# A LoRA kernel that streams its input through SBUF: loads and stores regrouped into six parts of 2, 6, 8, 16, 16 and 16 tiles

## The chip, the core and the metric

The kernel runs on one core of one Trainium2 chip. The metric is device time in microseconds (us) of one execution; a lower one is better. The kernel before took 125.18 us, the median of 3 runs (125.13 to 125.36).

## The reference: what is computed

```python
def setup_inputs():
    batch, seq, d_model, r = 16, 512, 768, 16
    ...
        "x": np.random.randn(batch, seq, d_model).astype(np.float32),
        "A": np.random.randn(d_model, r).astype(np.float32) * 0.1,
        "B": np.random.randn(r, d_model).astype(np.float32) * 0.1,
        "scale": 0.5,
...
    lora = np.matmul(np.matmul(x, A), B)
    return (x + scale * lora).astype(np.float32)
```

The input x has 8192 rows of 768 float32 numbers, which is 25.17 MB, and the output has as many. Every byte of x is read once and every byte of the output is written once; A and B have 48 KB each.

## The kernel before, in words

**Tiles, parts and chunks.** The 8192 rows are 64 tiles of 128 rows. The whole of x stays in one SBUF tensor `xs` of 128 partitions by 64 tiles by 768 numbers. The result is added into `xs` in place, and the stores take it from there. `LOADS` (line 13) groups the tiles into eight loads of 2, 2, 4, 8, 8, 8, 16 and 16 tiles. `rows` (line 69) lays a group of n tiles out so that each partition holds n rows which follow each other in DRAM: a load of 16 tiles is 128 runs of 48 KB, one to a partition. `STORES` (line 14) has ten stores of 2, 2, 4, 8, 8, 8, 8, 8, 8 and 8 tiles in the order of the tiles. Each of the last four is half of a 16-tile group, so it is 128 runs of 24 KB that lie 48 KB apart in DRAM.

**The queue.** All loads and stores are issued by SyncE (SP) into one hardware queue, which is served in order by 16 DMA engines. SP issues loads 0 and 1, then waits until a patch of SBUF is cleared (`zeroed`), issues the loads of A and B, then loads 2 to 6. The last load waits for `prep` (line 116), since A and B are staged in its space (line 64). Then SP goes through the stores: each waits until VectorE has counted `added` up (line 122), so that its tiles are summed.

**The work of a chunk.** Computing goes in 16 chunks of 4 tiles.
- `narrowed` (line 85) casts a third of the chunk (256 of the 768 columns) from float32 to float16 into `xh`; VectorE does thirds 0 and 1, ScalarE third 2. It waits for the landing of each load that holds a tile of the chunk, the first time that its engine needs that load.
- `turned` (line 181): TensorE transposes `xh` into PSUM by matmuls with the identity, six times for a chunk.
- ScalarE copies each transposed piece out of PSUM into `xt` (line 136).
- `projected` (line 192): TensorE multiplies by A, and ScalarE scales the result into `yt` (line 140).
- `expanded` (line 200): TensorE multiplies `yt` by B, for one tile, into one of two PSUM buffers.
- `summed` (line 145): VectorE adds that to the tile in `xs`; after the last tile of each store it drains and counts `added`.

**Order on each engine.** It is written out by hand. TensorE's first chunk waits for `prep` between its first three transposes and its first projection (line 227); then a loop runs over the chunks, each with the expansion of the chunk before it between its own steps. VectorE first casts two thirds of chunk 0, then transposes A and makes the float16 copies of A and B, which end with `prep` (line 165); in each later round it casts thirds 0 and 1 of the next chunk and sums the four tiles of the chunk before. ScalarE casts third 2 of the next chunk after the six copies of this one. POOL waits at the end until all stores have landed (line 129).

Of the kernel before, what the change touches and what calls it, by code (L numbers as in the profile page):

```python
# [9 lines left out]
MM_DT = mybir.dt.float16  # L10


LOADS = [2, 2, 4, 8, 8, 8, 16, 16]
STORES = [2, 2, 4, 8, 8, 8, 8, 8, 8, 8]

CHUNK = 4

# [2 lines left out]
def kernel(  # L20
# [8 lines left out]
    nc = tc.nc  # L29
    fp32 = mybir.dt.float32  # L30
    add = mybir.AluOpType.add
    P = 128

    x2 = x.flatten_outer_dims()
    out2 = out.flatten_outer_dims()
    T, D = x2.shape
    R = A.shape[1]
    NT = T // P
# [3 lines left out]
    NX = 3  # L42
    W = 2 * P
    NB = D // 32
    assert D % W == 0 and sum(LOADS) == NT == sum(STORES)
    n_splits = [(n0, min(512, D - n0)) for n0 in range(0, D, 512)]
    sc = float(scale)

    sb = ctx.enter_context(tc.tile_pool(name="sb", bufs=1))
    ps = ctx.enter_context(tc.tile_pool(name="ps", bufs=1, space=bass.MemoryType.PSUM))  # L50

    xs = sb.tile([P, NT, D], fp32, name="xs")
    ident = sb.tile([P, P], MM_DT, name="ident")
    a_mm = sb.tile([P, ND, R], MM_DT, name="a_mm")
    b_mm = sb.tile([R, D], MM_DT, name="b_mm")
    xh = [sb.tile([P, CHUNK, W], MM_DT, name=f"xh{u}") for u in range(NU)]
    xt = [sb.tile([P, CHUNK * P], MM_DT, name=f"xt{j}") for j in range(ND)]
    yt = sb.tile([R, CHUNK * P], MM_DT, name="yt")
    xt_ps = [ps.tile([P, CHUNK * P], fp32, name=f"xt_ps{b}") for b in range(NX)]
    yt_ps = ps.tile([R, CHUNK * P], fp32, name="yt_ps")  # L60
# [2 lines left out]

    room = NT - LOADS[-1]
    a_rows = xs[0:32, room, 0 : 32 * R].rearrange("b (a r) -> b a r", r=R)
    a_t = xs[0:32, room + 1, 0 : 32 * R].rearrange("a (r b) -> a r b", r=R)
    b_f32 = xs[0:R, room + 2, :]

    def rows(t2, t0, n):
        return t2[ds(t0 * P, n * P), :].rearrange("(p s) d -> p s d", s=n)  # L70

    with tc.tile_critical():  # L72
        names = "zeroed ident a b a_t prep fed0 fed1 fed2 turned got proj y lora freed added".split()
        S = {k: nc.alloc_semaphore(name=f"s_{k}") for k in names}
        landed = [nc.alloc_semaphore(name=f"s_load{i}") for i in range(len(LOADS))]
        stored = nc.alloc_semaphore(name="s_stored")
        part_of = [i for i, n in enumerate(LOADS) for _ in range(n)]

        def load(i):
            t0, n = sum(LOADS[:i]), LOADS[i]  # L80
            nc.sync.dma_start(out=xs[:, t0 : t0 + n, :], in_=rows(x2, t0, n)).then_inc(landed[i], 16)
# [3 lines left out]
        def narrowed(engine, c, u):  # L85
            for i in sorted({part_of[c * CHUNK + s] for s in range(CHUNK)}):
                if (engine.engine, i) not in known:
                    known.add((engine.engine, i))
                    engine.wait_ge(landed[i], 16)
            src = xs[:, ds(c * CHUNK, CHUNK), ds(u * W, W)]  # L90
            if engine is nc.scalar:
                i = engine.copy(out=xh[u], in_=src)  # L92
            else:
                i = engine.tensor_copy(out=xh[u], in_=src)  # L94
            i.then_inc(S[f"fed{u}"], 1)
# [6 lines left out]
            out=ident, in_=ident, compare_op=mybir.AluOpType.not_equal, fill=1.0,  # L102
# [8 lines left out]
            out=a_rows[0:NB, :, :], in_=A.rearrange("(b a) r -> b a r", a=32)  # L111
        ).then_inc(S["a"], 16)
        nc.sync.dma_start(out=b_f32, in_=B).then_inc(S["b"], 16)
        for i in range(2, len(LOADS) - 1):
            load(i)
        nc.sync.wait_ge(S["prep"], 1)
        load(len(LOADS) - 1)
        done = 0
        for k, n in enumerate(STORES):
            i = part_of[done]  # L120
            t0, w = sum(LOADS[:i]), LOADS[i]
            nc.sync.wait_ge(S["added"], k + 1)
            piece = slice(done - t0, done - t0 + n)
            nc.sync.dma_start(
                out=rows(out2, t0, w)[:, piece, :], in_=xs[:, done : done + n, :]
            ).then_inc(stored, 16)
            done += n

        nc.gpsimd.wait_ge(stored, 16 * len(STORES))


        narrowed(nc.scalar, 0, 2)
        for c in range(NC):
            for j in range(ND):
# [2 lines left out]
            if c + 1 < NC:  # L137
# [3 lines left out]
                out=yt, in_=yt_ps, func=mybir.ActivationFunctionType.Copy, scale=sc  # L141
# [8 lines left out]
            if k + 1 in ends:  # L150
                nc.vector.drain().then_inc(S["added"], 1)  # L151

        ends = {sum(STORES[: i + 1]) for i in range(len(STORES))}
        nc.vector.sem_inc(S["freed"], 2)
        narrowed(nc.vector, 0, 0)
        narrowed(nc.vector, 0, 1)
# [110 lines left out]
```

## Time and profile before

| what | value |
|---|---|
| median of 3 runs | 125.18 us |
| the profiled execution: its own time | 125.31 us |
| its span in the trace | 123.5 us |
| VectorE busy / TensorE matmul busy / ScalarE busy | 80.2 / 84.3 / 76.2 us |
| DMA packets, bytes, mean rate | 2662, 50.45 MB, 408 GB/s |
| first load issued / first store issued | 0.94 us / 21.39 us |
| last store issued / landed | 101.2 us / 122.5 us |

The profile shows one execution, with times from the start of its span. A DMA instruction on SP is short, since it only issues; the transfer is seen in the DMA rows and in the time from issue to landing. The DMA share of a stretch is the time that the packets starting in it took, as a share of the 16 engines. A packet here is one run of one partition, so a packet of 48 KB that starts near the end of a stretch counts wholly in that stretch, and single stretches of a microsecond swing around their mean. In a list of waits, "A <- B" says that A waited for B.

### The profile page before, as it was taken

Reading aid. Unit: us, or ns where it says so; the run is one execution under the profiler, and the core shown is the slowest. Engines: PE = TensorE matmul, PEld = TensorE weight load, DVE = VectorE, ACT = ScalarE, POOL = GpSimd, SP = SyncE. Lnnn points to the kernel's source line nnn. Section 1 sums busy time; section 2 is a strip of 40 time slices with the busy share of each in tenths; the row PEclk is TensorE's granted clock in tenths of the full one; section 3 lists DMA queues with packets and bytes.
Section 4 is the critical chain, followed back from the end, with each engine's and each line's share of the span. In section 5 each row is a group of like instructions: output and inputs, shape, how many; then the busy total and the mean of one; then the engine's idle time right before and its main releaser. Section 6 shows DMA issues by size and latency. Waiting matters only on the chain. (4 is left out here: it accounts for less than half of the span.)

```text
span 123.5 us, 1804 instructions
## 1 busy us (share of the span) xinstructions
PE 84.3 (68%) x608; PEld 39.7 (32%) x608; DVE 80.2 (65%) x102; ACT 76.2 (62%) x129; POOL 1.1 (1%) x7
## 2 busy tenths in 40 slices
PE   0024986999999999999999999999999420000000
PEld 0022342444445444454444544445444100000000
DVE  0049208888999999999899999999977770000000
ACT  0047598469889898898988989889896100000000
POOL 3000000000000000000000000000000000000000
PEclk9999999589999999999999999999999975555555
DMA  3999999999999699899889999999999999999990
GB/s 86 414 396 426 477 398 454 422 406 469 414 509 477 302 496 493 382 401 477 288 366 448 434 477 398 446 438 398 477 398 446 438 398 485 390 454 438 390 414 16
DMA packets 2662, 50.45 MB, mean 408 GB/s; under 512 B 316, under 2 KB 316, under 8 KB 868
## 3 DMA queue, kind: packets, MB, share of 16 engines
q1 hardware_dynamic: 2660, 50.43, 96.4%
q14 instruction: 2, 0.02, 0.0%
HBM read 25.26 MB, written 25.17 MB: 408 GB/s over the span
## 5 line engine op out<-in xcount | busy, mean ns | idle before, releaser
L147 DVE TENSOR_TENSOR xs<-xs,lo_ps 128x768 f32<-128x768 f32 x64 | 58.1, 950 | 5.5 <-PE lo_ps L205 4.8
L136 ACT CAST xt<-xt_ps 128x512 f16<-128x512 f32 x96 | 52.4, 577 | 10.1 <-PE xt_ps L186 8.4
L186 PE MATMUL xt_ps<-ident,xh 128*128 128x128 f16 x384 | 34.4, 229 | 8.6 <-PEq L179 8.6
L194 PE MATMUL yt_ps<-xt,a_mm 128*16 128x512 f16 x96 | 32.9, 396 | 1.8 <-PEq L179 1.6
L94 DVE CAST xh<-xs 128x1024 f16<-128x1024 f32 x32 | 22.0, 689 | 15.3 <-DMA xs<-in_x_dram 13.1
L186 PEld LDWEIGHTS xt_ps<-ident,xh 128*128 128x128 f16 x384 | 23.0, 102 | 26.9 <-issue 26.9
L205 PE MATMUL lo_ps<-b_mm,yt 16*128 16x512 f16 (+1 forms) x128 | 26.6, 324 | 5.4 <-PEq L179 3.5
L92 ACT CAST xh<-xs 128x1024 f16<-128x1024 f32 x16 | 16.8, 1048 | 0.0
L205 PEld LDWEIGHTS lo_ps<-b_mm,yt 16*128 16x128 f16 x128 | 9.6, 92 | 15.2 <-issue 9.5
L194 PEld LDWEIGHTS yt_ps<-xt,a_mm 128*16 128x16 f16 x96 | 7.1, 87 | 17.8 <-issue 13.0
L140 ACT ACTIVATE yt<-yt_ps 16x512 f16<-16x512 f32 x16 | 9.4, 587 | 2.6 <-PE yt_ps L194 2.6
L92 ACT ACT_TABLE_LOAD x1 | 1.3, 1283 | 7.8 <-DMA xs<-in_x_dram 7.8
L159 DVE STREAM_TRANSPOSE xs<-xs 32x512 f32<-32x512 f32 x1 | 1.0, 1037 | 0.0
L163 DVE CAST a_mm<-xs 32x96 f16<-32x96 f32 x4 | 0.9, 231 | 0.1
L165 DVE CAST b_mm<-xs 16x768 f16<-16x768 f32 x1 | 0.5, 548 | 0.0
L98 POOL MEMSET xs<- 32x512 f32 x1 | 0.5, 514 | 0.5 <-SPq L72 0.5
L101 POOL TENSOR_SCALAR_AFFINE_SELECT ident<-ident 128x128 f16<-128x128 f16 x1 | 0.3, 292 | 0.2 <-POOL ident L99 0.2
L99 POOL MEMSET ident<- 128x128 f16 x1 | 0.2, 194 | 0.0
L248 POOL MEMSET const-bfloat16-1.0<- 128x1 bf16 x1 | 0.1, 101 | 0.0
L248 POOL MEMSET const-uint8-127<- 128x1 uint8 x1 | 0.1, 101 | 0.0
L248 POOL MEMSET const-float32-0.0<- 128x1 f32 x1 | 0.1, 98 | 0.2 <-issue 0.2
L248 POOL MEMSET const-float32-1.0<- 128x1 f32 x1 | 0.1, 98 | 0.0
## 6 DMA issues: line engine op xcount, KB each, us to landing
out_dram<-xs SPq DMA_DIRECT2D x7, 3072.0 KB, 29.4
xs<-in_x_dram SPq DMA_DIRECT2D x2, 6144.0 KB, 48.0
xs<-in_x_dram SPq DMA_DIRECT2D x3, 3072.0 KB, 22.3
xs<-in_x_dram SPq DMA_DIRECT2D x2, 768.0 KB, 5.3
xs<-in_x_dram SPq DMA_DIRECT2D x1, 1536.0 KB, 8.8
out_dram<-xs SPq DMA_DIRECT2D x2, 768.0 KB, 44.2
out_dram<-xs SPq DMA_DIRECT2D x1, 1536.0 KB, 41.5
xs<-in_A_dram SPq DMA_DIRECT2D x1, 48.0 KB
```

Of the source, the lines that this page charges most:

```text
L92: i = engine.copy(out=xh[u], in_=src)
L94: i = engine.tensor_copy(out=xh[u], in_=src)
L98: nc.gpsimd.memset(a_rows, 0.0).then_inc(S["zeroed"], 1)
L136: nc.scalar.copy(out=xt[j], in_=xt_ps[j % NX]).then_inc(S["got"], 1)
L140: nc.scalar.activation(out=yt, in_=yt_ps, func=mybir.ActivationFunctionType.Copy, scale=sc).then_inc(S["y"], 1)
L147: nc.vector.tensor_tensor(out=xs[:, k, :], in0=xs[:, k, :], in1=lo_ps[k % 2], op=add).then_inc(S["freed"], 1)
L159: nc.vector.transpose(out=a_t, in_=a_rows.rearrange("b a r -> b r a")).then_inc(S["a_t"], 1)
L163: nc.vector.tensor_copy(out=a_mm[ds(32 * k, 32), :, :], in_=a_tv[:, k, :, :])
L165: nc.vector.tensor_copy(out=b_mm, in_=b_f32).then_inc(S["prep"], 1)
L186: i = nc.tensor.matmul(xt_ps[j % NX][:, ds(s * P, P)], xh[u][:, s, ds(h * P, P)], ident, start=True, stop=True,)
L194: i = nc.tensor.matmul(yt_ps, a_mm[:, j, :], xt[j], start=(j == 0), stop=(j == ND - 1))
L205: i = nc.tensor.matmul(lo_ps[s % 2][:, ds(n0, w)], yt[:, ds(s * P, P)], b_mm[:, ds(n0, w)], start=True, stop=True,)
```

## The change

- The tiles are grouped into six parts of 2, 6, 8, 16, 16 and 16 tiles. In each part a partition holds as many rows as the part has tiles, all next to each other in DRAM.
- There are seven loads: 2, 6, 8, 8, 8, 16 and 16 tiles. Part 3 (tiles 16 to 31) is loaded as two halves of 8 tiles, each 128 runs of 24 KB that lie 48 KB apart. The first chunk's four tiles come with loads 0 and 1 as before, and load 1 now has 6 tiles in place of 2. A and B are still issued after load 1, and the last load still waits for `prep`.
- There are six stores, each of a whole part, in the order 3, 0, 1, 2, 4, 5. The first (tiles 16 to 31) waits until four parts are summed, tiles 0 to 31; the stores of parts 0, 1 and 2 follow it without a wait; parts 4 and 5 wait for their own sums.
- VectorE drains and counts `added` six times in place of ten.
- ScalarE gets a first instruction: when the identity is made, it copies one column of it to a small tile that nothing reads.

```diff
-LOADS = [2, 2, 4, 8, 8, 8, 16, 16]
-STORES = [2, 2, 4, 8, 8, 8, 8, 8, 8, 8]
+PARTS = [2, 6, 8, 16, 16, 16]
+LOADS = [2, 6, 8, 8, 8, 16, 16]
+STORES = [3, 0, 1, 2, 4, 5]
...
+    first = sb.tile([P, 1], MM_DT, name="first")
...
+    starts = [sum(PARTS[:i]) for i in range(len(PARTS))]
+
     def rows(t2, t0, n):
-        return t2[ds(t0 * P, n * P), :].rearrange("(p s) d -> p s d", s=n)
+        i = max(i for i in range(len(PARTS)) if starts[i] <= t0)
+        part = t2[ds(starts[i] * P, PARTS[i] * P), :].rearrange("(p s) d -> p s d", s=PARTS[i])
+        return part[:, ds(t0 - starts[i], n), :]
...
-        done = 0
-        for k, n in enumerate(STORES):
-            i = part_of[done]
-            t0, w = sum(LOADS[:i]), LOADS[i]
-            nc.sync.wait_ge(S["added"], k + 1)
-            piece = slice(done - t0, done - t0 + n)
+        summed_parts = 0
+        for i in STORES:
+            t0, n = starts[i], PARTS[i]
+            if i + 1 > summed_parts:
+                summed_parts = i + 1
+                nc.sync.wait_ge(S["added"], summed_parts)
             nc.sync.dma_start(
-                out=rows(out2, t0, w)[:, piece, :], in_=xs[:, done : done + n, :]
+                out=rows(out2, t0, n), in_=xs[:, t0 : t0 + n, :]
             ).then_inc(stored, 16)
-            done += n
-
         nc.gpsimd.wait_ge(stored, 16 * len(STORES))
 
 
+        nc.scalar.wait_ge(S["ident"], 1)
+        nc.scalar.copy(out=first, in_=ident[:, 0:1])
         narrowed(nc.scalar, 0, 2)
...
-        ends = {sum(STORES[: i + 1]) for i in range(len(STORES))}
+        ends = {sum(PARTS[: i + 1]) for i in range(len(PARTS))}
```

More of the change, by code (lines that the diff above doesn't have):

```diff
@@ L44 @@
     NB = D // 32
-    assert D % W == 0 and sum(LOADS) == NT == sum(STORES)
+    assert D % W == 0 and sum(LOADS) == NT == sum(PARTS) and sorted(STORES) == list(range(len(PARTS)))
     n_splits = [(n0, min(512, D - n0)) for n0 in range(0, D, 512)]
```

## The prediction

> **What bounds the kernel now.** I read the page's DMA rows first, then the SP queue's instructions, then the time from issue to landing.
>
> ```profile
> DMA  3999999999999699899889999999999999999990
> q1 hardware_dynamic: 2660, 50.43, 96.4%
> ```
>
> The 16 DMA engines are busy from end to end: 96.4% of 123.5 us is 119.1 us. The digit 6 is no hole: the trace's packet records, laid end to end into 16 chains (the next packet starts within some 10 ns of the last one's end), have no gap over 30 ns between 2.0 and 120 us. The queue is served in order, so the chains are loads until about 62 us and stores after that. The issues show how far SP is ahead:
>
> ```profile
> 21.39 80.11 SPq L124 DMA_DIRECT2D out_dram<-xs  x10
> ...
> 60.96 0.33 SPq L124 DMA_DIRECT2D out_dram<-xs  x1
> ...
> 101.18 0.33 SPq L124 DMA_DIRECT2D out_dram<-xs  x1
> ```
>
> The first store is issued at 21.39 us and lands 44.5 us later, at 65.9, since all loads are ahead of it. The sixth (tiles 24 to 31) is issued at 60.96, the last at 101.18; that one lands 21.3 us later, at 122.5, and the span ends 1.04 us after it. So computing is 21 us ahead at the end, and what counts is the number of bytes, the rate, and whether an engine ever finds its queue empty. The last question is where this change acts.
>
> **When the sixteen engines leave the loads.** By the chains, twelve end their last load packet at 61.7 to 62.3 us, two at 62.7, one at 63.0, and the last at 63.86. From there to the last store packet takes 58.27 us on an ordinary chain (62.173 to 120.434). Two chains end late, at 122.03 and 122.12. One is that which left the loads at 63.86. The other left them early, at 61.9 or before, but is slow while storing: its 24 KB packets take 945 to 1001 ns against 912, until 95.5 us, when computing is nearly over. Its stores take about 60.14 us (61.893 to 122.030).
>
> **The start of the work.** Moved loads act here.
>
> ```profile
> 7.75 1.28 ACT L92 ACT_TABLE_LOAD   x1 [7.75 <-DMA xs<-in_x_dram]
> 7.78 1.29 DVE L94 CAST xh<-xs 128x1024 f16<-128x1024 f32 x2 [7.78 <-DMA xs<-in_x_dram]
> ...
> 11.04 0.55 DVE L165 CAST b_mm<-xs 16x768 f16<-16x768 f32 x1
> ...
> 11.69 0.59 PE L194 MATMUL yt_ps<-xt,a_mm 128*16 128x512 f16 x1 [1.63 <-PEq L179]
> ...
> 18.90 0.69 DVE L94 CAST xh<-xs 128x1024 f16<-128x1024 f32 x1 [5.35 <-DMA xs<-in_x_dram]
> ```
>
> Chunk 0 starts at 7.78, when tiles 2 and 3 have landed. VectorE's casts and its work on A and B end with `prep` at 11.59 (3.81 us later), and TensorE's first projection starts at 11.69. Later VectorE is idle for 5.35 us, until tiles 8 to 15 land: that is the only slack in front. From then on computing runs at a fixed pace: the stores of 8 tiles are issued at 40.36, 50.66 and 60.96, 10.30 apart, or 5.15 us for a chunk, with ScalarE, TensorE and VectorE each over 90% busy in 20 to 60 us. A delay that is left at 20 us is still there at 60.
>
> **The change, part by part.**
>
> *Fewer, longer packets.* An ordinary chain's stores of 2, 4 and 8 tiles follow each other at 1.86, 3.65 and 7.27 us by their landings; a 16-tile load took 14.53. Twice the size costs twice the time but for 0.02 to 0.08 us a transfer. Stores before: 2 x 1.86 + 3.65 + 7 x 7.27 = 58.26; after: 1.86 + 5.46 (3.65 and 7.27 halved in between) + 7.27 + 3 x 14.53 = 58.18. Loads save 0.05 in the same way. Gain: 0.1 to 0.15 us, on the path. Whole runs in DRAM bring nothing more: 24 KB runs 48 KB apart (stores 7 to 10) land 7.27 apart, just as contiguous ones do (stores 4 to 6).
>
> *Load 1 of 6 tiles.* The four-tile load of before lands 8.8 us after its issue at 2.73, at 11.5; by then tiles 0 to 7 and A and B have passed. The 6-tile load ends with the same bytes less the 0.1 MB of A and B (0.23 us at 420 GB/s): 11.25. Chunk 0 starts 3.5 us later, `prep` comes at 15.1, the first projection at 15.2, chunk 1's transposes at 19.5 (16.02 before). Cover: VectorE now comes to tiles 8 to 15 at about 20.1, when they have lain there since 18.8, so 1.2 us of the 3.5 is left at that point. Chunk 1 then runs without that stall, in some 5.6 us against 7.2, and chunk 2 in 5.15 against 5.93 (the granted clock fell to 0.5 from 21.97 to 25.38 there), so chunk 3 starts at about 30.3 instead of 29.14. **Delay: 1.2 us**; from below 0.8 (a landing at 10.9), from above 2.5, since the warm-up is not certain: matmuls of 512 columns took 0.60 us up to 15.1 and 0.38 after, that is 3.4 us after 11.69. If the same step comes a whole stretch of 3.4 us later, rounds of 1.07 us stand for rounds of 0.64, 0.4 us for each us, 1.4 in all. I take 1.2, the value that repeats the row.
>
> *ScalarE's early copy.* It moves the table load of 1.28 us from 7.75 to about 2. Before, its copies ended at 11.55 beside `prep` at 11.59; after, projections wait for `prep` at 15.1 anyway, and the copies end about 14.2. Worth 0; without that cover, 1.28.
>
> *Four drains less.* 0.87 us is the longest (the last, which ends the chain of waits); in mid-work VectorE isn't the one that others wait for. Taken at 0, with 0 to 0.2 in favour.
>
> *The first store.* Four stores that stood in the queue from 21 to 51 us, and a fifth and a sixth, become one that SP holds until tile 31 is summed: 60.96 + 1.2 = 62.15 us. It is the longest wait, and behind it on SP stand three stores that need nothing. From issue to the first packet on an empty queue took 1.02 us at the start (0.94 to 1.96), so packets flow at **63.2 us**. Bounds: 0 if the queue were never empty, 1.3 with the fill seen at the start, where first packets took 0.4 to 0.9 us for 0.23. Most engines have had nothing to do since about 61.9: 1.3 us lost on each. The engine that left the loads at 63.86 loses nothing, and its last packet (2.78 us against 1.82, as stores of others ran beside it) should be shorter.
>
> On issuing early, the Trainium skill speaks against this change: "DMA: Bandwidth & Descriptors", Rules for kernel authors, would have a DMA issued early so that its fixed cost overlaps. Its figure of about 2.0 us of fixed cost is for the other descriptor path; with that for my 1.02 the sum would be an estimated 1 us later. The same section would join small transfers into large ones; here ten stores land back to back, so no fixed cost shows that joining could save.
>
> *The end.* Parts 0 to 2 follow at once. Part 4 is summed at 81.5 + 1.2, when the queue has work until 63.2 + 14.5 + 14.6 = 92.3; part 5 at 102.4, plus 1.0, with work until 106.8. Cover: 3.4 us; no second hole. Should the delay reach 4.6, it opens.
>
> **The sum.** The slow storing chain: 63.2 + 60.14 - 0.08 = 123.2 for its last packet, landing 0.42 later as before (122.03 to 122.45), span end 1.04 after that: 124.7. The profiled execution's own time stands 1.77 over its span (125.31 to 123.54): 126.4. It was 0.13 over the median: **126.3 us**, 0.9% slower.
>
> **Rivals.**
>
> 1. *The gap is taken from engines that had time to spare (faster).* The chain that left the loads at 63.86 set the end too, and for it the store was never late. If the slow storing chain is slow only in the profiled execution (its excess ends with computing, and the page can't tell the cause), all engines begin at 63.2 and end 58.2 later, at 121.4; landing 0.4 and 1.04 more: 122.85, which gives 124.5; with 0.1 to 0.2 for filling, **124.6 us**. For: by the chains, eleven engines are done by 120.6 us and have some 1.5 us to spare at the end. Against: equal profiled and unprofiled times, which fit the slow chain being always there too. It decides for faster as long as the first packet flows before about 63.8.
> 2. *It comes out even.* As rival 1, but the delay is 1.7 to 2.2 us from a late warm-up: the gap eats the spare 0.6 us. **125.2 us.**
> 3. *Clock lost in front as well.* Slow chain as in the forecast and a delay of 2.5: 126.3 + 1.3 = **127.6 us**; without the slow chain, 125.9.
> 4. *The regrouping does nothing*, because a lead of loads or compute I overlook keeps the queue full: 125.18 - 0.15 = **125.0 us**. Against: 60.96 against 61.9 leaves SP 0.9 us, less than the 1.02 from issue to packet even with no delay.
>
> **Chances and range.** Forecast and rival 3 (both slower): 0.42 and 0.16. Rival 1: 0.26. Rivals 2 and 4: 0.11 and 0.05. About 0.2%, 0.25 us, is what a measurement of this kernel can tell from no change. Rival 4 and half of the edges of rival 2 fall inside that: faster 0.28, same 0.14, slower 0.58. The range goes from rival 1's 124.6 less 0.1 to 127.4, which leaves out the worst of rival 3. The forecast's own range is 125.7 to 127.0.
>
> **What would show it.** Right: SP's first store at 62 to 63 us; the DMA rows with a hole there, of about 1 us on most engines; chunk 0's casts at 11.3; no wait of VectorE for tiles 8 to 15; the last store landing about 60.5 us after the first packet. Wrong: chains that end together at 121.4, with no slow one (rival 1); a first store before 61 (rival 4); a granted clock of 0.5 or 0.60 us matmuls beyond 19 us (rivals 2 and 3); a second hole at 104 to 107.

## The result, and the profile after

The changed kernel took 126.24 us, the median of 7 runs (126.09 to 126.84), against 125.29 us for the kernel before (7 runs, 125.11 to 125.83). The ratio is 1.0081, with a 95% interval of 1.0063 to 1.0099: slower by 0.8%. The profiled execution had a span of 125.1 us and took 126.84 us, 0.6 us above the median, which the reading has to allow for. The ratio of each experiment below is to executions of the kernel before taken beside it; a few executions (3 of 12 in one run) fell into a slower state at a lower granted clock, and the medians below count them while the ratios leave them out.

The page's DMA rows and the SP queue's instructions after the change:

```profile
DMA  3999999999999979989595995999899699959960
...
q1 hardware_dynamic: 1940, 50.43, 94.8%
```
```profile
62.70 40.75 SPq L131 DMA_DIRECT2D out_dram<-xs  x6
...
103.11 0.33 SPq L131 DMA_DIRECT2D out_dram<-xs  x1
```

1940 packets in place of 2660 moved the same 50.43 MB, and the engines' time is the same: 94.8% of 125.06 is 118.6 us, 96.4% of 123.54 was 119.1. What grew is the time beside it, from 4.4 to 6.5 us. The first store is now issued at 62.70 us. The digits 5 and 6 late in the row don't show where it went, since a 48 KB packet is counted where it starts. Single microseconds around the hole do (the last two columns are the engines' share and GB/s); first the changed kernel, then the two middle ones in the kernel before:

```profile
60.00:61.00 1.00, 1.00 (x9) 0.45 (x8) 0.74 (x2) 0.94 (x3) 0.00 (x0) 1.00 0.68 295
61.00:62.00 1.00, 1.00 (x9) 0.43 (x9) 1.00 (x2) 1.00 (x2) 0.00 (x0) 1.00 0.01 0
62.00:63.00 1.00, 0.86 (x13) 0.59 (x11) 0.86 (x2) 1.00 (x3) 0.00 (x0) 1.00 0.00 0
63.00:64.00 1.00, 1.00 (x9) 0.44 (x7) 1.00 (x2) 0.87 (x2) 0.00 (x0) 1.00 1.87 786
```
```profile
61.00:62.00 1.00, 0.99 (x5) 0.37 (x5) 0.98 (x2) 1.00 (x3) 0.00 (x0) 1.00 0.29 98
62.00:63.00 1.00, 1.00 (x10) 0.54 (x9) 1.00 (x2) 0.64 (x2) 0.00 (x0) 1.00 0.77 320
```

After the change no data packet starts from 61 to 63, then 16 of 48 KB at once; before, packets start in both microseconds. By the packet chains fourteen engines leave the loads at 61.3 to 62.1, the others at 62.3 and 62.8, and all begin to store at 63.54 to 63.69, 0.85 us or more after the issue: each was idle for 0.9 to 2.2 us. The list of waits puts it on VectorE's sums (lines 151 and 158 are the drain after them); the kernel before first:

```profile
SPq L124 <- DVEq L151: 86.0, 10, 10.0
```
```profile
SPq L131 <- DVEq L158: 84.0, 3, 47.0
```

There are three waits where there were ten, and one of 47.0 us. Their total, 86.0 before and 84.0 now, says nothing: SP waits all the time in both kernels, and only in one are the DMA engines out of work meanwhile.

The front, from the timeline, answers to the lines shown of before:

```profile
0.90 1.28 ACT L138 ACT_TABLE_LOAD   x1 [0.90 <-SPq L79]
...
11.54 1.29 DVE L101 CAST xh<-xs 128x1024 f16<-128x1024 f32 x2 [11.54 <-DMA xs<-in_x_dram]
...
15.44 0.58 PE L201 MATMUL yt_ps<-xt,a_mm 128*16 128x512 f16 x1 [1.62 <-PEq L186]
...
20.01 1.46 PE L193 MATMUL xt_ps<-ident,xh 128*128 128x128 f16 x12
...
21.08 0.69 DVE L101 CAST xh<-xs 128x1024 f16<-128x1024 f32 x1 [3.79 <-PE xt_ps L193]
...
30.88 0.84 PE L193 MATMUL xt_ps<-ident,xh 128*128 128x128 f16 x12
```

Chunk 0 starts at 11.54 in place of 7.78 and the first projection at 15.44 in place of 11.69. VectorE's idle time before the casts of chunk 2 (line 101) is now 3.79 us and ends with TensorE, no longer with the DMA. The twelve transposes at 20.01 took 1.46 us, those at 30.88 took 0.84: the TensorE clock came up at 21.76, later than in the trace of before (15.1). Chunk 3 starts 1.74 us later than before (30.88 to 29.14), and 62.70 is 1.74 later than 60.96: what is lost at 30 us arrives unchanged at the first store.

The last line is in the tail, the same view:

```profile
120.00:121.00 1.00, 0.00 (x0) 0.00 (x0) 0.00 (x0) 0.00 (x0) 0.00 (x0) 0.50 1.71 737
121.00:122.00 1.00, 0.00 (x0) 0.00 (x0) 0.00 (x0) 0.00 (x0) 0.00 (x0) 0.50 0.11 49
```

49 GB/s in a microsecond is one packet of 48 KB. Fifteen engines start their last packet from 120 to 121 (737 is 15 x 49.15), one starts its own after 121. It is the slowly storing chain: fifteen land by 122.49, the last at 124.02.

### The profile page after: what moved, and what is told of

The parts are those of the page before. It is cut to its first block, busy times and chain, and to the rows that moved or that the text cites. A ratio compares the mean times of both kernels' runs of the same rounds, so it can differ in the third digit from the quotient of the medians.

```text
span 125.1 us, 1795 instructions
## 1 busy us (share of the span) xinstructions
PE 84.3 (67%) x608; PEld 39.7 (32%) x608; DVE 80.3 (64%) x102; ACT 76.5 (61%) x130; POOL 1.2 (1%) x7
## 3 DMA queue, kind: packets, MB, share of 16 engines
q1 hardware_dynamic: 1940, 50.43, 94.8%
```

## The experiments

Theory: the loss is the hole between loads and stores, made by two things together: computing starts 3.6 to 3.8 us later, and the first store waits for tile 31. Rivals: the regrouping (whole 16-tile parts, the six-tile load) costs by itself; holding stores back costs by itself; engines have time to spare, so the hole is mostly free. Each edit is to the changed kernel unless said otherwise.

**Natural order.** The stores no longer wait for tile 31.

```diff
-STORES = [3, 0, 1, 2, 4, 5]
+STORES = [0, 1, 2, 3, 4, 5]
```

> The changed kernel with its six stores in the order of the tiles (0, 1, 2, 3, 4, 5), so that the first is issued at about 24 us and stands in the queue behind the loads. Theory (what costs is the hole between loads and stores): no hole, and the time is that of the kernel before less 0.1 us of packets: 125.0 to 125.3 us, although computing still starts 3.5 us later. Rival (whole 16-tile parts, or the six-tile load, cost by themselves): 126.2 us, as with the change.

Measured: 125.19 us, ratio to before 0.9989 (0.9975 to 1.0002). The SP queue's instructions:

```profile
23.26 79.47 SPq L131 DMA_DIRECT2D out_dram<-xs  x6
```

Computing starts as late as in the change (chunk 0's casts at 11.35) and it costs nothing, since the first store is in the queue at 23.26. Whole parts, the six-tile load and the late start by themselves cost nothing that shows; the first rival falls.

**The kernel before, with its stores held.** An edit to the kernel before:

```diff
-            nc.sync.wait_ge(S["added"], k + 1)
+            nc.sync.wait_ge(S["added"], max(k + 1, 6))
```

> The kernel before with one edit: its stores wait until 32 tiles are summed, and the first six are then issued together, at about 61 us. Theory: packets flow at 61.9 us, when most engines have just left the loads, so the hole is at most 0.2 us on the chain that stores slowly: 125.2 to 125.5 us. Rival (holding the stores back costs by itself, whenever it ends): 126.2 us or more.

Measured: 125.19 us, ratio 0.9986 (0.9972 to 1.0001). The SP queue's instructions:

```profile
59.65 40.55 SPq L124 DMA_DIRECT2D out_dram<-xs  x10
```

The first store was issued at 59.65 us, before any engine had left the loads, so no hole came. Holding the stores back costs nothing that shows as long as it ends in time; the second rival falls.

**The front of before, stores still held.**

```diff
-PARTS = [2, 6, 8, 16, 16, 16]
-LOADS = [2, 6, 8, 8, 8, 16, 16]
-STORES = [3, 0, 1, 2, 4, 5]
+PARTS = [2, 2, 4, 8, 16, 16, 16]
+LOADS = [2, 2, 4, 8, 8, 8, 16, 16]
+STORES = [4, 0, 1, 2, 3, 5, 6]
```

> The changed kernel with the first eight tiles as parts of 2, 2 and 4 again, and seven stores of whole parts, still with tiles 16 to 31 first. Theory: computing starts at 7.8 us again, the first store is issued at 61 us instead of over 62, and 1 us comes back: 125.1 to 125.5 us. Rival (the order of the stores, or whole 16-tile parts, cost): 126.2 us.

Measured: 124.96 us, ratio 0.998 (0.9955 to 1.0006); first store at 59.66. As the theory has it.

**Only the load of part 1 undone.** Parts and stores stay; part 1 is loaded in pieces of 2 and 4 tiles.

```diff
-LOADS = [2, 6, 8, 8, 8, 16, 16]
+LOADS = [2, 2, 4, 8, 8, 8, 16, 16]
```

> The changed kernel with parts and stores as they are, but part 1 loaded in two pieces of 2 and 4 tiles, so that chunk 0 can start at 7.8 us again. Theory (the front's delay, handed on to the held first store, is the whole loss): 124.8 to 125.2 us, with the first store issued at 59.7 to 61 us. Rival (something else of the change costs, which the front of before in the run with seven stores had hidden): 125.6 us or more.

Measured: 125.05 us, ratio 0.9977 (0.9964 to 0.999), so 0.2% faster than before and, by the two ratios, 1.0% faster than the change: the whole loss is gone. The SP queue's instructions, and the same single microseconds:

```profile
59.89 1.78 SPq L131 DMA_DIRECT2D out_dram<-xs  x3
```
```profile
61.00:62.00 1.00, 1.00 (x11) 0.56 (x10) 1.00 (x2) 0.64 (x2) 0.00 (x0) 1.00 1.27 541
62.00:63.00 1.00, 1.00 (x9) 0.53 (x9) 0.98 (x2) 0.89 (x3) 0.00 (x0) 1.00 0.57 246
```

Packets start in both stretches in which the changed kernel had none. The first store comes 2.81 us earlier than in the change, and the profiled time falls by 1.79 (126.84 to 125.05): the rest of the lead only waits in the queue. Whether tiles 2 to 7 come in one load or in two is the difference between an exposed and a hidden hold.

**The front of before, natural order.** As the run with seven stores, but:

```diff
-STORES = [4, 0, 1, 2, 3, 5, 6]
+STORES = [0, 1, 2, 3, 4, 5, 6]
```

> The regrouped kernel with the front of before, parts of 2, 2, 4, 8, 16, 16 and 16 tiles, and its seven stores in the order of the tiles. Tells apart what made 124.96 us of the same parts with tiles 16 to 31 first. If holding the stores back is neutral, both are the same: 124.9 to 125.2 us. If it helps the loads that end last, this one is slower by 0.2 to 0.3 us.

Measured: 125.11 us, ratio 0.9989 (0.9976 to 1.0002). The order of the stores moves the time by no more than this measurement tells: 124.96, 125.05 and 125.11 lie within 0.15 us.

**One chunk later.** The dose: the first store waits for 36 tiles.

```diff
-                nc.sync.wait_ge(S["added"], summed_parts)
+                nc.sync.wait_ge(S["added"], summed_parts + 1)
...
-        ends = {sum(PARTS[: i + 1]) for i in range(len(PARTS))}
+        ends = {sum(PARTS[: i + 1]) for i in range(len(PARTS))} | {36}
```

> The changed kernel with its first store held until 36 tiles are summed, one chunk more. Theory: every engine's hole is 5.15 us longer, and so is the time: 131.2 to 131.6 us. Rival (engines have time to spare, so a hole counts only in part): under 130.5 us.

Measured: 131.17 us, at the lower edge of what was expected and 4.93 more than the change. The SP queue's instructions:

```profile
67.40 35.61 SPq L131 DMA_DIRECT2D out_dram<-xs  x6
```

Between the two profiles the first store moved by 4.70 (62.70 to 67.40), the last landing of the fifteen ordinary engines by 4.69 (122.49 to 127.18), and the span by 4.42; the difference of 0.28 is the slow chain, which ends 1.26 us after the others in place of 1.53, with less computing beside it. For the fifteen the hole counts in full; no time to spare is left, and the third rival falls.

**Without ScalarE's early copy.**

```diff
-        nc.scalar.wait_ge(S["ident"], 1)
-        nc.scalar.copy(out=first, in_=ident[:, 0:1])
         narrowed(nc.scalar, 0, 2)
```

> The changed kernel without ScalarE's early copy, so the table load of 1.28 us stands again between the landing and ScalarE's first cast. Theory: ScalarE's first copies still end before TensorE's first projection is let go by VectorE's work on A and B, so nothing moves: 126.1 to 126.4 us. Rival (the early load is on the path): 127.3 to 127.6 us.

Measured: 126.38 us, ratio to before 1.009 (1.0055 to 1.0124); the change's 1.0081 lies within. From the timeline of ScalarE:

```profile
11.57 1.28 ACT L98 ACT_TABLE_LOAD   x1 [11.57 <-DMA xs<-in_x_dram]
```

The table load stands behind the landing again, and the first store is issued at 62.69 against 62.70: it is not on the path.

**All stores held to the end,** so that storing has no computing beside it.

```diff
-                nc.sync.wait_ge(S["added"], summed_parts)
+                nc.sync.wait_ge(S["added"], len(PARTS))
```

> The changed kernel with every store held until all 64 tiles are summed, at about 102.7 us, so that storing has no computing beside it. If the one slow chain is slow because of computing beside it, all sixteen engines end within 0.3 us of each other, 58.2 us after the first packet: 165.0 us. If that engine stores slowly by itself, one is late by 1.8 us again: 166.8 us.

Measured: 165.06 us. In the tail, by single microseconds:

```profile
159.00:160.00 1.00, 0.00 (x0) 0.00 (x0) 0.00 (x0) 0.00 (x0) 0.00 (x0) 0.50 1.37 590
160.00:161.00 1.00, 0.00 (x0) 0.00 (x0) 0.00 (x0) 0.00 (x0) 0.00 (x0) 0.50 0.46 197
161.00:162.00 1.00, 0.00 (x0) 0.00 (x0) 0.00 (x0) 0.00 (x0) 0.00 (x0) 0.50 0.01 0
```

590 and 197 are 12 and 4 packets: all sixteen engines, and none later. Their last landings lie between 162.07 and 162.24. So the slow chain is slow because something computes beside it.

**Many small matmuls, few wide ones.** A kernel that only copies x through SBUF (the LoRA term is left out); beside its stores TensorE runs a loop, in the second kernel with `WIDE` 512 and 12 rounds:

```python
WIDE, ROUNDS = 128, 48
...
        with nc.Fori(0, ROUNDS, engines=(mybir.EngineType.PE,)):
            for k in range(16):
                nc.tensor.matmul(
                    xt_ps[k % 2][:, 0:WIDE], ident, xh[:, 0:WIDE], start=True, stop=True
                )
```

> Only copies x through SBUF (the LoRA term is left out); stores start when all loads have landed, and beside them TensorE alone works, on 768 matmuls of 128 columns with as many weight loads, for about 50 us. If the slow chain comes from the number of instructions that TensorE executes, its 24 and 48 KB packets are longer by 9% or more here, against some 5% in the changed kernel, and it ends more than 3 us late. If it comes from VectorE or ScalarE, no chain is slow.

> The same copy with 192 matmuls of 512 columns, about as long in all but a quarter of the instructions. By number of instructions: the slow chain's packets are longer by 2 to 4% and it ends about 1 us late. By TensorE's busy time or the data that it reads: the same lateness as with the 768 small ones.

Measured: 128.83 and 125.99 us. TensorE was busy for nearly the same time (the page's first part of each):

```profile
PE 44.4 (35%) x768; PEld 44.3 (35%) x768; POOL 0.9 (1%) x6
```
```profile
PE 43.5 (35%) x192; PEld 19.2 (15%) x192; POOL 0.9 (1%) x6
```

Beside the small ones one chain's 48 KB packets took 1980 to 2008 ns against 1820 (9 to 10% more), and it landed 3.34 us after the other fifteen. Beside the wide ones they took 1848 to 1873 ns (1.5 to 3% more), and it landed 0.58 us late, less than the 1 us expected. So the slowness goes with the number of instructions rather than with the busy time of the matmuls. The busy time of the weight loads (PEld) fell too, from 44.3 to 19.2 us, and this pair doesn't separate it; the next run, which has no weight loads, shows that they can't be all of it.

**VectorE and ScalarE alone.** The same copy with 256 tiny copies on each, and no matmul.

```python
            for k in range(ROUNDS):
                if engine is nc.scalar:
                    engine.copy(out=dst[:, 4 * k : 4 * k + 4], in_=xh[:, 0:4])
                else:
                    engine.tensor_copy(out=dst[:, 4 * k : 4 * k + 4], in_=xh[:, 0:4])
```

> The copy of x alone (the LoRA term is left out), with 256 tiny copies on VectorE and 256 on ScalarE beside the stores, and no TensorE work. If any executed instruction delays the slow chain, by the 2.0 ns each that the small matmuls and weight loads gave, it ends about 1.0 us late. If only TensorE's do, all sixteen engines end within 0.3 us of each other.

Measured: 127.06 us, and the last engine landed 1.50 us after the thirteenth. It isn't TensorE alone: while both engines worked, one chain's 24 KB packets again took 954 to 982 ns. But the size isn't clean: the trace also has four packets of instruction fetch (8 KB, 0.31 us each) among the stores, and two further engines ended 0.7 and 1.0 us late.

**Relieving one engine (failed).** An attempt to take work off the slow chain, on the kernel with seven stores: part 0's store is cut into 120 and 8 partitions.

```diff
-            nc.sync.dma_start(
-                out=rows(out2, t0, n), in_=xs[:, t0 : t0 + n, :]
-            ).then_inc(stored, 16)
+            for p0, p1 in ((0, 120), (120, P)) if i == 0 else ((0, P),):
+                nc.sync.dma_start(
+                    out=rows(out2, t0, n)[p0:p1, :, :], in_=xs[p0:p1, t0 : t0 + n, :]
+                ).then_inc(stored, 16)
```

> The regrouped kernel with the front of before (parts of 2, 2, 4, 8, 16, 16, 16 tiles, tiles 16 to 31 first), which took 124.96 us, with the store of part 0 cut in two: 120 partitions and 8 partitions. Each engine has 8 partitions of a whole store; if 120 partitions go to fifteen engines and 8 to eight, the sixteenth has nothing to do in this part (1.86 us), and eight others 0.23 us more. If the slow chain is the sixteenth engine, its lead of 1.1 us over the next one goes: 123.9 to 124.3 us. If it is another one, or if shares are dealt out otherwise: 124.9 to 125.3 us.

Measured: 126.27 us, ratio 1.009 (1.0062 to 1.0117), slower than both expectations. While the cut store ran, 6 KB packets took up to 872 ns in place of 234. The rows of that stretch, the cut store first, then the uncut one of the kernel with seven stores:

```profile
77.00:78.00 1.00, 1.00 (x10) 0.52 (x9) 1.00 (x2) 0.94 (x2) 0.00 (x0) 1.00 0.86 276
78.00:79.00 1.00, 1.00 (x9) 0.41 (x7) 0.75 (x2) 0.94 (x3) 0.00 (x0) 1.00 1.05 344
```
```profile
77.00:78.00 1.00, 1.00 (x10) 0.49 (x9) 1.00 (x2) 0.88 (x3) 0.00 (x0) 1.00 0.98 406
78.00:79.00 1.00, 1.00 (x6) 0.37 (x5) 0.74 (x2) 1.00 (x2) 0.00 (x0) 1.00 1.00 412
```

The engines are about as busy but move less. Which engine is the slow one stays open, and so does why a store of 120 partitions runs so unevenly.

## Why the prediction was right, point by point

It gave 126.3 us and the median is 126.24. The mechanism was the right one, but that the number came so close is in part luck, as shown below. Its terms, against the profiled execution:

| step | predicted | in the trace |
|---|---|---|
| chunk 0 starts | 11.25 to 11.3 | 11.54 |
| first projection | 15.2 | 15.44 |
| chunk 3 starts | 30.3 | 30.88 |
| first store issued | 62.15 | 62.70 |
| issue to first packet | 1.02 | 0.85 |
| first packet | 63.2 | 63.54 |
| slow chain, first packet to landing | 60.5 | 60.48 |
| span's end after that | 1.04 | 1.04 |
| profiled time | 126.4 | 126.84 |
| median | 126.3 | 126.24 |

**Fewer packets: 0.1 to 0.15 predicted, not shown.** The four regrouped kernels without a hole took 124.96 to 125.19 us, 0.12 to 0.35 less than the runs of before beside them, and only the run with part 1 in two loads has an interval that excludes 1. But the kernel before with its stores held has all the old packets and stood 0.12 lower as well (125.19 against 125.31).

**The delay: right mechanism, mis-sized by 0.55 in this execution.** Of it some 0.25 is the landing. The rest is put down to the clock, whose price the step had as its upper bound; the matmuls at the lower clock beyond 19 us, which the prediction named as a sign of rivals 2 and 3, were there. The step to full clock came at 21.76 here, at 21.67 without the early copy and at 20.76 with the store one chunk later; less that chunk, the first stores stood at 62.70, 62.69 and 62.25, which is 0.44 us for 1.0 us of later clock, near the 0.4 estimated. The natural-order run fits (clock at 20.04, the store that ends with tile 31 issued at 61.97), the run with all stores held doesn't: its clock came at 19.18, and yet tile 31 was summed at 62.15, as with the step at 20.76 (62.18). So a later clock can be part of the delay, but its price stays open. It can't be shown for the median's run, which has no trace here, but 126.24 less the same terms (1.77, 1.04, 60.48, 0.85) puts its first store at 62.1, within these 61.97 to 62.70. One reading in this step was wrong: ScalarE was busy for 34.19 of the 40 us from 20 to 60, or 85%, not over 90%. The fixed pace of 5.15 us for a chunk, which the step used, holds all the same.

**A mistake that cancelled.** The step took the trace of before as the norm for that front. Four other profiles with the same front issue their first held store at 59.65 to 59.97, not 60.96; none of them has the fall to clock 0.5 at 21.97. So the true delay between the two fronts is 2.0 to 3.1 us (61.97 to 62.70 against these), not 1.2: the slack in VectorE's idle time covers only 0.7 to 1.6 us of the 3.6 to 3.8. That the sum still came out was luck: it needs only the end of the loads and the issue after the change, and for the second the trace of before happened to be late by the size of that error. Rival 4's argument fails with it: a held store of the old front does come in time. Rival 3's delay of 2.5 us lies within the measured 2.0 to 3.1, but its 127.6 us counts it from the same late 60.96.

**Early copy, four drains: right, 0.** For the copy a run without it shows it, though the table load moved to 0.90 us, not to about 2; the drains were not tried by themselves.

**The first store and the end: right.** The hole is there, idle time of 0.9 to 2.2 us on each engine, and the run one chunk later shows that it counts in full. No second hole opened: the last store was issued at 103.11, when the store ahead of it still had 4.7 us to run until its first landing at 107.78.

**Rivals 1 and 2 were wrong on the slow chain.** It is in every profile that has computing beside the stores, and none of the change's seven executions took less than 126.09 us. The other fifteen engines did end together, as rival 1 said, but at 122.1 us, 0.7 later than its 121.4.

## What to carry to other kernels

In a stream that one queue serves in order, issue the next transfer while the last one still runs: being early changed nothing here (a first store at 23 or at 60 us), and each microsecond by which the first store missed the end of the loads cost one. Before holding a transfer back or coarsening a first load, follow the start of computing through to the wait that the held transfer stands on, and compare with when the engines leave the work ahead of it, not with the last landing. Take that lead from several executions: in one trace it was 1.0 to 1.3 us shorter than in four others.

## What the runs showed of the hardware that was not expected

- One of the sixteen DMA engines stores more slowly while other engines execute instructions. From the first store on, the lateness of its last landing and the instructions recorded on TensorE, VectorE and ScalarE were: 1.53 us for 753 (the change), 1.26 for 647 (one chunk later), 3.34 for 1639 (small matmuls), 0.58 for 415 (wide ones), and nothing for a handful (all stores held). That is 1.4 to 2.0 ns for each. The run with VectorE and ScalarE alone gives more, 1.50 for 527, but has the instruction fetches among its stores. Whether the instructions do it or their recording by the profiler, these runs can't tell. The Trainium skill ("DMA: Bandwidth & Descriptors", Latency and other measured facts) has it that two of the engines are usually slower in traces, and guesses at the descriptor rings that GpSimd's DMAs use; here SP issued every load and store, one engine was slow, and only beside computing.
- In the eleven profiles with all of the computing the TensorE clock stepped to full speed 3.4 to 6.4 us after the first projection (11.69 to 15.14 in before, 15.44 to 21.76 in the change, 11.99 to 18.35 in the kernel with the cut store), and in one of them, that of before, it fell back to 0.5 for 3.4 us.
